# Up tiles of the SwiGLU parts as block products, and another place for the w_ada dot products

## The chip, the core and the metric

The kernel runs on one core of a Trainium2 chip. The core's engines work side by side, each on its own instruction stream: TensorE (PE; its weight loads are listed apart as PEld), VectorE (DVE), ScalarE (ACT), GpSimd (POOL) and SyncE (SP, which issues nearly all DMAs here). The metric is device time in microseconds. A profiled execution gives a trace beside it.

## What is computed

Two layers of a streaming encoder on x of 512 positions by 1024 features, all in float32. Each layer has three sub-layers, each behind a norm whose shift, scale and gate come from the vector c:

```python
c_act = silu(c)
for l in range(2):
    mod = (c_act @ w_ada[l] + b_ada[l]).reshape(B, 9, 1024)
    h = modulate(rms_norm(x, norm_gain[l, 0]), mod[:, 0], mod[:, 1])
    x = x + 0.5 * mod[:, 2] * swiglu(h, w_gate[l, 0], w_up[l, 0], w_down[l, 0])
    h = modulate(rms_norm(x, norm_gain[l, 1]), mod[:, 3], mod[:, 4])
    x = x + mod[:, 5] * hybrid_mixer(h, ...)
    h = modulate(rms_norm(x, norm_gain[l, 2]), mod[:, 6], mod[:, 7])
    x = x + 0.5 * mod[:, 8] * swiglu(h, w_gate[l, 1], w_up[l, 1], w_down[l, 1])

def swiglu(h, w_gate, w_up, w_down):
    return (silu(h @ w_gate) * (h @ w_up)) @ w_down
```

w_gate and w_up are 1024 x 2816, w_down is 2816 x 1024. The mixer has three branches (A: attention with a learned bias, B: pooling over trailing windows, C: attention with forget gates); each branch's output goes through its own matrix and a sigmoid gate that is itself a product of h, the three are summed, and an output product follows. `mod` is 9216 dot products of length 1024 in each layer.

## The kernel before

**Numbers in two halves.** Each float32 operand of a product is split into a high half (a rounded copy, made by ScalarE) and a low half (the rest, one subtraction on VectorE). `triple` (line 117) then does three matmuls for one product: high by high, high by low, low by high.

**Weights.** `wchunk` (262) brings one 512 KB weight tile: a load into one of two "raw" buffers from SP's queue, the split into one of three "whi" tiles on ScalarE (277) and one of three "wlo" tiles on VectorE (279).

**SwiGLU.** `Ffn.run` (595) handles the 22 tiles of 128 hidden features in three parts of 6, 8 and 8 tiles. Each part makes its hidden tiles ("acts") from gate and up products, then its share of the down product (`k_outer`, 388) with the residual in `residual_tail` (430). A tile of gate or up done alone is `unit` (577): 8 x 3 matmuls of 512 columns. In parts 1 and 2, gate tiles go in pairs through `seven` (507): the pair's weights are seen as 2 x 2 blocks and so is h, and seven block products stand for eight, by Winograd's form of Strassen's scheme. That is 7 x 4 x 3 = 84 matmuls of 256 columns for two tiles (`add_product`, lines 128 to 130). Beside them it needs sums of weight blocks (522 to 525), their splits, and folds of partial results (538 to 549) in a tile "c". The sums and "c" live in the four buffers tagged "v2" (the profile writes "v"). The sums of h's blocks are made once for each sub-layer by `Blocks` (454), during part 0. The up tiles go through `seven` only where there is no next phase (`nxt is None`), that is in the last SwiGLU of layer 1; in the other three they are two `unit`s.

**The w_ada dot products.** `mod_step` (200) does 128 of the 9216 outputs of a layer: a 512 KB load from SP's queue into a "v2" buffer, one multiply-and-sum against silu(c) on VectorE (206), and one small instruction for a scale or a gate. silu(c), spread over all partitions, lies in `silc`, a "b" buffer. There are 144 steps; 16 are done in the kernel's first product, and 128 stand in `mod_queue`. They are taken out at a rate: each weight tile asks `side_work` (251) first.

```python
elif side and in_ffn[0] and mod_tag[0] == "v2":
    mod_credit[0] += MOD_RATE[0]
    while mod_credit[0] >= 1.0:
        mod_credit[0] -= 1.0
        mod_pop()
```

So nothing is taken while `in_ffn` is false (the mixer) or the tag is "raw" (the down product of a SwiGLU's last part). `mod_need(l, j)` (231) takes out at once what is still missing up to output group j of layer l. It is called where results are needed: by each phase's `prefetch` (the next phase's norm), and ahead of each down product (its gate).

**The mixer.** `Mixer.run` (1114): projections, attention A, attention C with the merge of branch A as filler, then branch B's `pool_front` (1025) four times and the merge of branch C (`merge_units`, 1068), the merge of branch B, and the output product. Branch C's values lie in the four "v2" buffers until its attention ends, and the low and high halves of the merged result take them from the merge of branch B on. GpSimd adds the branches up (1149). In layer 0, `silc` is loaded again after the attentions (1168 to 1170); in layer 1 it is not.

**Order.** The program states each engine's instructions; a scheduler puts them in a fixed order for each engine ahead of the run, ready instructions by their place in the program. A "b" tile takes one of 17 buffers.

Of the kernel before, what the change touches and what calls it, by code (L numbers as in the profile page):

```python
# [15 lines left out]
F32 = mybir.dt.float32  # L16
# [6 lines left out]
P = 128  # L23
T = 512
D = 1024
# [3 lines left out]
L = 2  # L29
# [11 lines left out]
def encoder_kernel(tc, xT, c, w_ada, b_ada, gains, w_gate, w_up, w_down, w_qkv, w_f, w_ubg,  # L41
                   qk_gain, rel, fbias, w_pool, pool_scale, w_branch, w_out, inv_cnt, w_first, out):
    nc = tc.nc
# [14 lines left out]
    NB, NRAW = 17, 2  # L58
# [5 lines left out]
    def st(shape, dt, tag, bufs):  # L64
        return sb.tile(shape, dt, tag=tag, bufs=bufs, name=nm(tag))
# [4 lines left out]
    def mmt(shape=(P, T)):  # L70
        return ps.tile(list(shape), F32, tag="mm", bufs=4, name=nm("mm"))
# [66 lines left out]
    silc = [st([P, D], F32, "b", NB)]  # L138
    sil_dram = dr.tile([1, D], F32, name="sil_dram")
# [84 lines left out]
    mod_tag = ["v2"]  # L224
# [6 lines left out]
    def mod_need(l, j):  # L231
        while mod_ptr[0] < min(len(mod_queue), (l * 9 + j + 1) * 8 - 16):
            mod_pop()

    MOD_RATE = [1.0]
    in_ffn = [True]
# [325 lines left out]
    class Ffn:  # L562
# [32 lines left out]
        def run(self, nxt):  # L595
            l, s, ms = self.l, self.s, self.ms
            in_ffn[0] = True
            mod_tag[0] = "v2"
            parts = ((0, 6), (6, 8), (14, 8))
            for part, (f0, nf) in enumerate(parts):  # L600
                acts = []
                n = 0
                if part == 0 and self.norm is None:
                    acts = self.start()
                    n = 3
                    blocks = Blocks()
                elif part == 0:
                    g0, u0, g1 = self.pre
                    pg, pu, pg1 = mmt(), mmt(), mmt()
                    for hs in range(2):  # L610
                        self.norm.back(hs, acc if hs else mmt)
                        cols = slice(hs * HALF, (hs + 1) * HALF)
                        if hs == 0:
                            later(FRONT1, lambda: self.norm.front(1, acc))
                            later(BACK1, lambda: self.norm.back(1, acc))
                        for k in range(KD):
                            self.unit(pg, g0, cols, (k,))
                            self.unit(pu, u0, cols, (k,))
                        self.unit(pg1, g1, cols)
                    u1 = self.gate_up(1, 1)  # L620
                    acts.append(self.act(0, pg, pu))
                    pu1 = mmt()
                    self.unit(pu1, u1)
                    acts.append(self.act(1, pg1, pu1))
                    n = 2
                    blocks = Blocks(self.norm.xa, modc[:, l, 3 * ms])
                if part == 0:
                    blocks.schedule(T_FIRST, T_STEP)
                elif part == 1:
                    blocks.finish()  # L630
                MOD_RATE[0] = 0.5 if part else 1.0
                while part and n < nf:
                    both = [apply(p, AF.Silu)
                            for p in seven([w_gate[l, s, f0 + n + i] for i in range(2)], blocks, acc)]
                    ups = seven([w_up[l, s, f0 + n + i] for i in range(2)], blocks, mmt) if nxt is None else None
                    for i, sg in enumerate(both):
                        if ups is not None:
                            pu = ups[i]
                        else:
                            u = self.gate_up(1, f0 + n + i)  # L640
                            pu = mmt()
                            self.unit(pu, u)
                        acts.append(self.act(n + i, None, pu, sg))
                    n += 2
                while n < nf:
                    g = self.gate_up(0, f0 + n)
                    u = self.gate_up(1, f0 + n)
                    pg, pu = mmt(), mmt()
                    self.unit(pg, g)
                    self.unit(pu, u)  # L650
                    acts.append(self.act(n, pg, pu))
                    n += 1
                mod_need(l, 3 * ms + 2)
                MOD_RATE[0] = 1.75
                for c0 in (0, T):
                    def src(c):
                        r0 = (f0 + 2 * c) * P
                        return w_down[l, s, r0:r0 + 2 * P, c0:c0 + T].rearrange("(k p) c -> p k c", p=P)

                    def ops(hi, lo, kt, j):  # L660
                        return (hi[:, j * P:(j + 1) * P], lo[:, j * P:(j + 1) * P],
                                acts[kt][:, 0, :], acts[kt][:, 1, :])

                    last = part == len(parts) - 1
                    if last and c0 == 0 and nxt is not None:
                        nxt.prefetch("v2")
                        mod_tag[0] = "raw"
                    split = last and c0 > 0
                    hook = None
                    if split:  # L670
                        hook = nxt.prefetch_weights if nxt is not None else (lambda: None)
                    for j, hs, o in k_outer(src, nf // 2, ops, hook):
                        d = c0 // P + j
                        residual_tail(d, hs, o, modc[:, l, 3 * ms + 2, d:d + 1], nxt if last else None)
                        if last and nxt is None:
                            cols = slice(0, T) if hs is None else slice(hs * HALF, (hs + 1) * HALF)
                            nc.sync.dma_start(out[:, d, cols], xd(d)[:, cols])
# [382 lines left out]
    def wpool_load(l):  # L1060
        raw = st([P, 4, P], F32, "t1", 2)
        nc.sync.dma_start(raw, w_pool[l].rearrange("g c e -> c g e"))
        w = st([P, 2, 4, P], F32R, "pta", 1)
        split_to(w[:, 0], w[:, 1], raw)
        return w[:, 0], w[:, 1]
# [32 lines left out]
    def drain(*gens):  # L1098
        for it in gens:
            for _ in it:  # L1100
                pass

    class Mixer:
# [1 line left out]
            self.l = l  # L1105

        def prefetch(self, xtag):
            mod_need(self.l, 5 if self.l + 1 < L else 8)
            self.norm = Norm(self.l, 1, xtag)

        def prefetch_weights(self):
# [2 lines left out]
        def run(self, nxt):  # L1114
# [50 lines left out]
            finish_turns()  # L1165
            turns.clear()
            poll(True)
            if l + 1 < L:
                silc[0] = st([P, D], F32, "b", NB)
                nc.sync.dma_start(silc[0], sil_dram.broadcast_to([P, D]))  # L1170
            wp = wpool_load(l)
            mc = merge_units(l, 2, yc, put_c)
            for gi in range(4):
                b = pool_front(l, gi)
                later(60, lambda gi=gi, b=b: pool_back(l, gi, b, wp, yb))
            drain(mc)
            poll(True)
            mb = merge_units(l, 1, yb, put_b)
            drain(mb)
# [87 lines left out]
```

## Time and profile before

| | |
|---|---|
| median of three runs | 2421.05 us (2418.97 to 2422.55) |
| span of the profiled execution | 2419.9 us |
| PE busy | 2380.5 us, 98% |
| VectorE busy | 1596.5 us, 66% |
| ScalarE busy | 1129.6 us, 47% |
| DMA | 320.27 MB, mean 132 GB/s |
| w_ada dot products (line 206) | 144, 188.0 us on VectorE |

A row of the profile that groups instructions gives the line of the kernel, the engine, the operation, what is written and what is read, shapes, a count, the busy time with the mean of one, and the idle time of the engine ahead of them with what ended it. A row in the order of time begins with start and length. A row of a stretch gives start and end, its length, then for each engine the busy time and the number of records, the granted TensorE clock, the DMA engines' busy share and GB/s. Matmuls are pipelined, so the distance of their starts tells their rate, not the length of one.

### The profile page before, as it was taken

Reading aid. Unit: us, or ns where it says so; the run is one execution under the profiler, and the core shown is the slowest. Engines: PE = TensorE matmul, PEld = TensorE weight load, DVE = VectorE, ACT = ScalarE, POOL = GpSimd, SP = SyncE. Lnnn points to the kernel's source line nnn. Section 1 sums busy time; section 2 is a strip of 40 time slices with the busy share of each in tenths; the row PEclk is TensorE's granted clock in tenths of the full one; section 3 lists DMA queues with packets and bytes.
Section 4 is the critical chain, followed back from the end, with each engine's and each line's share of the span. In section 5 each row is a group of like instructions: output and inputs, shape, how many; then the busy total and the mean of one; then the engine's idle time right before and its main releaser. Section 6 shows DMA issues by size and latency. Waiting matters only on the chain. (4 is left out here: it accounts for less than half of the span.)

```text
span 2419.9 us, 34577 instructions
## 1 busy us (share of the span) xinstructions
PE 2380.5 (98%) x13242; PEld 2061.8 (85%) x13242; DVE 1596.5 (66%) x2830; ACT 1129.6 (47%) x1946; POOL 342.8 (14%) x423
## 2 busy tenths in 40 slices
PE   7999999999999999999999999999999999999999
PEld 5888988778878898989898889888788888989898
DVE  8977756787643378777567766467866434658583
ACT  5342444786632353424443424457765333536362
POOL 3000001144432210000000000111454322000000
PEclk9999999999999999999999999999999999999999
DMA  7746443223323436464326443423233234133233
GB/s 272 243 157 235 158 137 98 93 70 111 104 91 113 139 98 242 158 235 157 131 79 214 171 163 105 140 70 101 86 100 104 96 108 145 65 100 103 95 103 104
DMA packets 116282, 320.27 MB, mean 132 GB/s; under 512 B 11122, under 2 KB 13298, under 8 KB 116116
## 3 DMA queue, kind: packets, MB, share of 16 engines
q1 hardware_dynamic: 114962, 313.86, 39.0%
q0 software_dynamic: 1152, 4.19, 0.4%
q8 instruction: 104, 1.70, 0.3%
q14 instruction: 62, 0.51, 0.1%
q10 hardware_dynamic: 2, 0.00, 0.0%
HBM read 311.64 MB, written 6.38 MB: 131 GB/s over the span
## 5 line engine op out<-in xcount | busy, mean ns | idle before, releaser
L277 ACT CAST whi<-raw 128x1024 fp32r<-128x1024 f32 (+1 forms) x315 | 327.7, 1044 | 573.5 <-PE acc L120 275.0
L279 DVE TENSOR_TENSOR wlo<-raw,whi 128x1024 fp32r<-128x1024 f32 x307 | 378.4, 1235 | 261.9 <-ACT whi L277 258.5
L119 PE MATMUL acc<-b,whi 128*128 128x512 f32 (+1 forms) x960 | 360.6, 376 | 0.0
L121 PE MATMUL acc<-b,wlo 128*128 128x512 f32 (+1 forms) x960 | 356.8, 372 | 0.8 <-DVE wlo L279 0.8
L120 PE MATMUL acc<-b,whi 128*128 128x512 f32 (+1 forms) x960 | 356.9, 372 | 0.0
L119 PE MATMUL mm<-hhi,whi 128*128 128x512 f32 x664 | 259.2, 391 | 1.4 <-ACT whi L277 1.4
L120 PE MATMUL mm<-hlo,whi 128*128 128x512 f32 x664 | 258.7, 390 | 0.0
L121 PE MATMUL mm<-hhi,wlo 128*128 128x512 f32 x664 | 258.1, 389 | 0.0
L206 DVE CUSTOM_DVE_ANT_0 v<-v,b,badac 128x1024 f32<-128x1024 f32 x144 | 188.0, 1316 | 32.9 <-DMA v<-in_w_ada_dram 32.7
L121 PEld LDWEIGHTS acc<-b,wlo 128*128 128x128 f32 x960 | 180.8, 188 | 32.6 <-DVE wlo L279 1.2
L119 PEld LDWEIGHTS acc<-b,whi 128*128 128x128 f32 x960 | 180.8, 188 | 31.6 <-DVE xv L434 0.3
L120 PEld LDWEIGHTS acc<-b,whi 128*128 128x128 f32 x960 | 180.9, 188 | 30.2
L119 PE MATMUL acc<-hhi,whi 128*128 128x512 f32 x480 | 191.0, 399 | 3.9 <-ACT whi L277 2.2
L120 PE MATMUL acc<-hlo,whi 128*128 128x512 f32 x480 | 188.3, 392 | 0.5 <-DVE hlo L717 0.5
L121 PE MATMUL acc<-hhi,wlo 128*128 128x512 f32 x480 | 188.0, 392 | 0.0
L119 PEld LDWEIGHTS mm<-hhi,whi 128*128 128x128 f32 x664 | 125.0, 188 | 27.5 <-ACT whi L277 2.3
L121 PEld LDWEIGHTS mm<-hhi,wlo 128*128 128x128 f32 x664 | 124.6, 188 | 26.2
L120 PEld LDWEIGHTS mm<-hlo,whi 128*128 128x128 f32 x664 | 124.7, 188 | 24.8
L119 PE MATMUL acc<-whi,hhi 128*128 128x512 f32 x336 | 137.8, 411 | 0.8 <-DVE xv L385 0.8
L121 PE MATMUL acc<-whi,hlo 128*128 128x512 f32 x336 | 132.0, 393 | 0.0
L120 PE MATMUL acc<-wlo,hhi 128*128 128x512 f32 x336 | 131.7, 392 | 0.0
L590 DVE TENSOR_TENSOR t<-mm,t 128x512 f32<-128x512 f32 (+1 forms) x78 | 51.7, 662 | 103.9 <-PE mm L121 102.6
(314 smaller groups left out, 5507.4 us busy)
## 6 DMA issues: line engine op xcount, KB each, us to landing
v<-in_w_ada_dram SPq DMA_DIRECT2D x144, 512.0 KB, 5.4
raw<-in_w_down_dram SPq DMA_DIRECT2D x88, 512.0 KB, 3.5
raw<-in_w_up_dram SPq DMA_DIRECT2D x82, 512.0 KB, 3.5
raw<-in_w_gate_dram SPq DMA_DIRECT2D x79, 512.0 KB, 3.8
raw<-in_w_ubg_dram SPq DMA_DIRECT2D x56, 512.0 KB, 3.4
raw<-in_w_qkv_dram SPq DMA_DIRECT2D x42, 512.0 KB, 3.7
raw<-in_w_branch_dram SPq DMA_DIRECT2D x24, 512.0 KB, 3.5
raw<-in_w_out_dram SPq DMA_DIRECT2D x16, 512.0 KB, 3.5
```

The source lines that it names most:

```text
L119: mm(o, lh, rh, start=start, stop=False)
L120: mm(o, lh, rl, start=False, stop=False)
L121: mm(o, ll, rh, start=False, stop=stop)
L206: dot = nc.vector.tensor_tensor_reduce(out=raw, in0=raw, in1=silc[0], scale=1.0, scalar=badac[:, l, j, d:d + 1], op0=ALU.mult, op1=ALU.add ...
L277: nc.scalar.copy(hi, raw)
L279: lo_eng.tensor_tensor(lo, raw, hi.bitcast(F32), op=ALU.subtract)
L590: nc.vector.tensor_tensor(pr[:, cols], p, sg[:, cols], op=ALU.mult)
```

## The change

In the three SwiGLU sub-layers that have a next phase, the up tiles of parts 1 and 2 now go in pairs through `seven` as well. The rate at which dot products are taken out goes from 0.5 to 0 in the gate and up products of parts 1 and 2, and from 1.75 to 1.25 in the down products; in part 0 it stays 1. The mixer's `prefetch` asks only for group 5 in both layers (before, group 8 in layer 1). `silc` is loaded again in layer 1 too. Around the pool fronts and the merge of branch C, `in_ffn` is true with rate 1, so that each of their weight tiles takes one dot product out.

```diff
-                MOD_RATE[0] = 0.5 if part else 1.0
+                MOD_RATE[0] = 0.0 if part else 1.0
                 while part and n < nf:
                     both = [apply(p, AF.Silu)
                             for p in seven([w_gate[l, s, f0 + n + i] for i in range(2)], blocks, acc)]
-                    ups = seven([w_up[l, s, f0 + n + i] for i in range(2)], blocks, mmt) if nxt is None else None
+                    ups = seven([w_up[l, s, f0 + n + i] for i in range(2)], blocks, mmt)
                     for i, sg in enumerate(both):
-                        if ups is not None:
-                            pu = ups[i]
-                        else:
-                            u = self.gate_up(1, f0 + n + i)
-                            pu = mmt()
-                            self.unit(pu, u)
-                        acts.append(self.act(n + i, None, pu, sg))
+                        acts.append(self.act(n + i, None, ups[i], sg))
                     n += 2
...
                 mod_need(l, 3 * ms + 2)
-                MOD_RATE[0] = 1.75
+                MOD_RATE[0] = 1.25
...
         def prefetch(self, xtag):
-            mod_need(self.l, 5 if self.l + 1 < L else 8)
+            mod_need(self.l, 5)
...
             poll(True)
-            if l + 1 < L:
-                silc[0] = st([P, D], F32, "b", NB)
-                nc.sync.dma_start(silc[0], sil_dram.broadcast_to([P, D]))
+            silc[0] = st([P, D], F32, "b", NB)
+            nc.sync.dma_start(silc[0], sil_dram.broadcast_to([P, D]))
             wp = wpool_load(l)
+            in_ffn[0] = True
+            mod_tag[0] = "v2"
+            MOD_RATE[0] = 1.0
             mc = merge_units(l, 2, yc, put_c)
...
             drain(mc)
+            in_ffn[0] = False
             poll(True)
```

## The prediction

> **What bounds the kernel now.** I read the page first, then the stretches of the SwiGLU parts, then their edges in the order of time, then the dot products in the same stretches, and last the waits.
>
> ```profile
> span 2419.9 us, 34577 instructions
> PE 2380.5 (98%) x13242; PEld 2061.8 (85%) x13242; DVE 1596.5 (66%) x2830; ACT 1129.6 (47%) x1946; POOL 342.8 (14%) x423
> PEclk9999999999999999999999999999999999999999
> ```
>
> PE is busy in 2380.5 of 2419.9 us, at an unchanged clock. So only less work on PE can shorten the kernel, and only a new gap on PE can lengthen it. The change touches six stretches, parts 1 and 2 of three SwiGLU sub-layers. The fourth sub-layer, the last one, already runs the form that the six are to get. Here are all eight in order, the last sub-layer in the last two rows.
>
> ```profile
> core 0: us, PE busy (x) PEld busy (x) DVE busy (x) ACT busy (x) POOL busy (x), PEclk, DMA share, GB/s
> 126.07:210.70 84.63, 83.78 (x529) 76.02 (x528) 64.29 (x100) 35.79 (x57) 0.00 (x0) 1.00 0.55 190
> 254.22:337.74 83.52, 83.52 (x529) 75.94 (x528) 55.94 (x83) 36.09 (x57) 0.00 (x0) 1.00 0.45 152
> 969.12:1052.64 83.52, 83.52 (x529) 75.94 (x528) 62.26 (x99) 35.53 (x57) 0.00 (x0) 1.00 0.56 190
> 1096.16:1179.68 83.52, 83.52 (x529) 75.94 (x528) 55.94 (x83) 35.75 (x57) 0.00 (x0) 1.00 0.44 153
> 1325.21:1410.18 84.97, 83.78 (x529) 76.01 (x528) 64.97 (x101) 35.77 (x57) 0.00 (x0) 1.00 0.54 187
> 1453.70:1537.22 83.52, 83.52 (x529) 75.94 (x528) 47.22 (x62) 35.61 (x57) 0.00 (x0) 1.00 0.33 109
> 2167.51:2247.83 80.32, 80.32 (x674) 79.96 (x672) 66.84 (x101) 46.70 (x81) 0.00 (x0) 1.00 0.36 112
> 2291.38:2371.46 80.08, 80.08 (x673) 79.95 (x672) 66.94 (x100) 46.65 (x81) 0.00 (x0) 1.00 0.36 113
> ```
>
> The first column is the length of the part's gate and up products. In a 528-matmul part, four pairs alternate 84 matmuls of 256 columns (gate) with 48 of 512 (up). In a 672-matmul part all eight groups are of 84. PE has no gap in any of them but the first and the fifth, whose gate product waits once for ScalarE's copy:
>
> ```profile
> 132.78 0.38 PE L128 MATMUL acc<-b,ptb 128*128 128x256 f32 x1 [0.85 <-ACT v L542]
> 1332.26 0.39 PE L128 MATMUL acc<-b,ptb 128*128 128x256 f32 x1 [1.19 <-ACT v L542]
> ```
>
> **The up tiles.** First and last starts of one gate group and one pair of up tiles, third part:
>
> ```profile
> 969.12 0.28 PE L128 MATMUL acc<-hhi,whi 128*128 128x256 f32 x1
> ...
> 979.10 0.40 PE L119 MATMUL mm<-hhi,whi 128*128 128x512 f32 x1
> ...
> 1052.64 0.39 PE L119 MATMUL acc<-b,whi 128*128 128x512 f32 x1
> ```
>
> A group of 84 takes 979.10 - 969.12 = 9.98 us, or 119 ns a matmul. The part of 83.52 us is four such groups and four times two up tiles, so these take (83.52 - 39.92) / 4 = 10.90 us, or 227 ns a matmul. Half a 512-column matmul would be 113.5 ns: seven products in place of eight promise 12.5%, but each short matmul costs some 5 ns extra, and the gain shrinks to 0.92 us a pair, 3.68 us a part. The last sub-layer shows what arrives of it: 83.52 - 80.32 = 3.20 us in its part 1 and 83.52 - 80.08 = 3.44 us in its part 2. I take these measured values rather than 3.68, since they hold the small delays that a fuller VectorE and ScalarE cause: 3 x 3.20 + 3 x 3.44 = **19.9 us less**. The first and fifth parts' excess (84.63 - 83.52 and 84.97 - 83.52, together 2.6 us) I leave where it is; if it went, the gain would be 22.5 us, the far end on that side.
>
> The row of the stationary loads in such a group is
>
> ```profile
> L128 PEld LDWEIGHTS acc<-b,ptb x384: 186/188/192, 128.8 to 2358.1; 128*128 128x128 f32 x192
> ```
>
> [...]
>
> **VectorE and ScalarE in those parts.** The seven products need sums, splits and folds that single tiles don't. By the table VectorE goes to 66.9 of 80 us, ScalarE to 46.7. This is hidden as long as VectorE has its 13 us left. The dots compete for just these:
>
> ```profile
> core 0: us, DVE busy (x), PEclk, DMA share, GB/s
> 126.07:210.70 84.63, 16.45 (x25) 1.00 0.55 190
> 254.22:337.74 83.52, 8.93 (x14) 1.00 0.45 152
> 969.12:1052.64 83.52, 15.50 (x25) 1.00 0.56 190
> 1096.16:1179.68 83.52, 9.01 (x14) 1.00 0.44 153
> ```
>
> A dot leaves two records, so about 12 dots lie in part 1 and 7 in part 2; one costs 1.3 us. With the rate at 0, only dots that the down product before left over run there: credit in part 1 was 8, so 4 of the 12 were leftovers, and at 1.25 in place of 1.75 fewer are. Four left over are 5 us of VectorE's 13. What can be late is the first up group of a part, prepared beside these leftovers: from nothing to one wait such as the two above (1.2 us), in three parts. I take nothing to 0.3 each, since the first gate group already shows that wait only twice in eight.
>
> **The dots' new places.** Counting credits by the code: 8 dots by the end of the first part 0, 15 and 25 after the next downs; then the mixer's prefetch needs 32, so 7 are issued at once at the end of part 2; the merges of branch C and its pool fronts have 16 weight chunks at rate 1, so 48; then 4 and 4 in part 0 as now (56), 64, 74; in layer 1's first sub-layer 4 and 2 (80), 87, 97, again 7 at once (104), 16 beside the merges (120), and 4 and 4 in part 0 of the last sub-layer (128). Each brings a 512 KB load on SP's queue.
>
> The 7 at once: their results are gates that only the output product uses, and the down product behind them is light. The nearest rows are the bulk that sub-layer two already has:
>
> ```profile
> 912.30 1.77 SPq L203 DMA_DIRECT2D v<-in_w_ada_dram  x4
> 917.08 0.38 SPq L266 DMA_DIRECT2D raw<-in_w_down_dram  x1
> 920.02 5.26 SPq L203 DMA_DIRECT2D v<-in_w_ada_dram  x4
> 925.37 0.39 SPq L266 DMA_DIRECT2D raw<-in_w_down_dram  x1
> ```
>
> and what PE and VectorE did around it (first row), beside VectorE's load in the down product after a part 2 (second) and in the merges of both layers (third, fourth):
>
> ```profile
> core 0: us, PE busy (x) PEld busy (x) DVE busy (x) ACT busy (x) POOL busy (x), PEclk, DMA share, GB/s
> 881.00:936.40 55.40, 55.40 (x272) 46.99 (x271) 46.88 (x73) 26.34 (x36) 0.00 (x0) 1.00 0.68 231
> 337.74:376.06 38.32, 38.32 (x236) 34.57 (x235) 17.50 (x20) 17.92 (x26) 8.44 (x8) 1.00 0.44 150
> 672.27:770.00 97.73, 97.73 (x432) 80.76 (x432) 39.21 (x49) 31.00 (x42) 29.09 (x29) 1.00 0.29 94
> 1870.72:1968.50 97.78, 97.78 (x433) 80.82 (x433) 39.31 (x49) 30.99 (x42) 29.09 (x29) 1.00 0.29 94
> ```
>
> Bursts of 4 loads between two weight loads, VectorE at 85%, 231 GB/s: no gap on PE. Seven dots (9 us) against 21 idle us of VectorE in the second row are hidden too; without that cover they would cost 9 us each time. I take 0.
>
> The merges: 16 dots are 21 us more on VectorE, 60 of 98, and 16 x 0.52 MB over 98 us is 86 GB/s more, 180 in all. Both are below the first row. The weights have slack there, since ScalarE's split waits not for the data but for PE to free the split tile:
>
> ```profile
> 714.94 1.05 ACT L277 CAST whi<-raw 128x1024 fp32r<-128x1024 f32 x1 [4.39 <-PE acc L120]
> 723.10 1.05 ACT L277 CAST whi<-raw 128x1024 fp32r<-128x1024 f32 x1 [6.61 <-PE acc L120]
> ```
>
> The dots' tiles ("v") hold branch C's values until the attention ends, so the first loads start just there, four at a time, among the pool fronts' weights. PE's wait at that spot is the same with a reload of the c vector (layer 0) and without it (layer 1, which gets it now):
>
> ```profile
> 669.19 0.63 PE L972 MATMUL mm<-ident,t 128*128 128x128 f32 x4 [1.52 <-DVE t L960]
> 1867.62 0.63 PE L972 MATMUL mm<-ident,t 128*128 128x128 f32 x4 [1.50 <-DVE t L960]
> ```
>
> So the reload is free. For the loads I take nothing to 1.5 us a layer, nearer to nothing. The 8 dots in the last sub-layer's part 0 meet what the first row above shows for the second sub-layer: 0. Lower rates in the downs take VectorE work out of gapless stretches: 0.
>
> **Sum.** Against the profiled execution: 2419.9 - 19.9 + 1 (starts of parts and merges together) = 2401 us of span. The median of the runs, 2421.05, lies 1.15 us above this span, so the forecast is **2402 us**; the small terms reach from 0 to 3 x 1.2 + 2 x 1.5 = 6.6 us, its own range is 2398 to 2408.
>
> **Rivals.** (B) *The edges leak.* Each of the six parts stalls its first up group by 1.2 us, and each merge phase by 1.5: 10.2 us in place of 1, **2411 us**. For it: the two waits quoted, in parts that begin with leftover dots. Against it: the last sub-layer shows none at either start.
>
> (C) *VectorE becomes the bound.* If all of the 12 dots of a part 1 stayed there, VectorE would have 66.9 + 16 = 83 us of work in an 80 us part, and the parts would take 83.5 us as now: **2421 us**, no change. This also stands for a change that doesn't thin out those parts as it says. Against it: rate 0 leaves leftovers alone.
>
> (D) *SP's queue, slower.* A dot's load waits at the head of SP's queue for a free "v" tile, and the weights of the merges queue behind it.
>
> ```profile
> SPq L203 <- DVE modc L206: 51.4, 33, 5.8
> ```
>
> Such waits exist: 33, 1.56 us on average. If each of the 32 loads beside the merges held up a weight chunk by that, uncovered, it would cost 50 us: 2421 - 20 + 50 = **2451 us**. It decides from 0.62 us uncovered a load (20/32). Against it: the 4.4 to 6.6 us that the splits wait for PE are cover for a wait of 1.56 and for most of 5.8.
>
> **Chances and range.** Forecast 0.74, B 0.15, C 0.05, D 0.06. What a measurement can tell from no change is 0.2%, or 4.8 us. Forecast and B are faster by more: 0.89; C is the same: 0.05; D is slower: 0.06. For eight in ten I take the forecast with its bounds and the nearer part of B: from 2397.5, a microsecond beyond the far end of 22.5 us gained, to 2412.
>
> **What would show it.** Six stretches of 672 matmuls and 80 to 81 us; groups of 84 at 9.98 us also in "mm" banks; no new PE wait over 1.5 us between 650 and 830 us nor in layer 1's merges; about 16 dots there; SP's waits before L203 longer without a PE wait behind them. I am wrong if a part with 672 matmuls takes over 82 us, if PE waits for L277 or L279 in the merges or after part 2, or if VectorE's idle time in those parts falls near nothing.

## The result, and the profile after

| | median us | lowest to highest | runs | span of the profiled execution |
|---|---|---|---|---|
| before | 2420.43 | 2418.11 to 2422.55 | 10 | 2419.9 |
| after | 2412.34 | 2408.73 to 2416.84 | 10 | 2410.1 |

The ratio is 0.9971, with a 95% interval of 0.9961 to 0.998: 8.1 us less by the medians, 9.8 us by the two spans. 2402 us was predicted, and 2397.5 to 2412 as the range. The page of after:

```profile
span 2410.1 us, 36817 instructions
PE 2363.2 (98%) x14106; PEld 2088.6 (87%) x14106; DVE 1729.5 (72%) x3070; ACT 1199.8 (50%) x2090; POOL 353.3 (15%) x423
PEclk9999999999999999999999999999999999999999
```

By this page nothing is wrong: PE is at 98% as before and the clock row reads 9 throughout. A slice of 60 us hides a few microseconds at half clock, as will be seen. The six parts with the new form, by stretches:

```profile
core 0: us, PE busy (x) PEld busy (x) DVE busy (x) ACT busy (x) POOL busy (x), PEclk, DMA share, GB/s
124.94:205.98 81.04, 80.32 (x674) 79.96 (x673) 70.24 (x107) 46.72 (x80) 0.00 (x0) 1.00 0.39 127
249.52:329.36 79.84, 79.84 (x674) 79.83 (x673) 70.04 (x108) 46.71 (x80) 0.00 (x0) 1.00 0.39 126
966.84:1046.67 79.83, 79.83 (x673) 79.82 (x672) 70.38 (x109) 46.89 (x80) 0.00 (x0) 1.00 0.41 133
1090.22:1170.15 79.93, 79.93 (x674) 79.89 (x672) 67.20 (x101) 46.92 (x81) 0.00 (x0) 1.00 0.34 117
1315.54:1395.59 80.05, 80.05 (x673) 79.88 (x672) 69.84 (x107) 46.79 (x80) 0.00 (x0) 1.00 0.38 128
1439.14:1519.11 79.97, 79.97 (x674) 79.89 (x672) 69.82 (x107) 46.80 (x80) 0.00 (x0) 1.00 0.37 126
```

They add up to 480.66 us, where the same six took 503.68: 23.0 us gained. Two parts of the last sub-layer, unchanged in form, give 0.7 more (79.83 us each). So some 14 us of 23.7 were lost again. Two rows of TensorE's timeline, one in each layer, carry most of it:

```profile
686.50 0.80 PE L121 MATMUL acc<-hhi,wlo 128*128 128x512 f32 x1 [3.95 <-DVE wlo L279]
1878.72 0.50 PE L121 MATMUL acc<-hhi,wlo 128*128 128x512 f32 x1 [3.91 <-DVE wlo L279]
```

Both lie beside the pool fronts, where the moved dots begin. First the same 27 us of layer 0 before, then after, with the two places at half clock:

```profile
672.27:699.50 27.23, 27.23 (x122) 22.42 (x122) 13.16 (x22) 10.46 (x16) 14.26 (x20) 1.00 0.27 86
```

```profile
663.24:690.50 27.26, 23.31 (x95) 18.77 (x95) 23.45 (x33) 9.69 (x15) 14.09 (x16) 0.90 0.64 238
685.30:692.10 6.80, 5.60 (x13) 4.44 (x14) 6.77 (x8) 2.75 (x4) 4.51 (x6) 0.50 0.47 167
1879.90:1883.30 3.40, 3.40 (x10) 2.63 (x9) 3.40 (x4) 0.69 (x1) 3.26 (x4) 0.50 0.76 299
```

PE was gapless there and is now idle for 4 us, while VectorE goes from 48% to 86%. At each wait the granted clock falls to 0.50, for 6.8 us in layer 0 and 3.4 us in layer 1. At half clock PE was busy for 5.60 + 3.40 us. Matmuls of 512 columns start 0.43 us apart there (layer 0, 687.09 to 691.36 us) and 0.23 us apart behind it (692.16 to 694.92), so by estimate half of that, 4.5 us, comes on top of the 7.9 us of waiting.

A third loss is in the down products after part 2. The one of layer 1 before, then both after:

```profile
1537.22:1575.53 38.31, 38.31 (x235) 34.56 (x234) 17.50 (x20) 17.92 (x26) 8.28 (x8) 1.00 0.44 148
```

```profile
329.36:368.89 39.53, 38.77 (x237) 34.68 (x235) 23.57 (x35) 18.55 (x27) 8.48 (x8) 1.00 0.62 212
1519.11:1559.10 39.99, 38.87 (x237) 34.70 (x236) 23.77 (x37) 18.56 (x27) 8.26 (x8) 1.00 0.61 210
```

They are 1.2 and 1.7 us longer. Here the chain does not start on VectorE. SP's queue in layer 0, and ScalarE's next split of a down weight:

```profile
318.64 12.40 SPq L203 DMA_DIRECT2D v<-in_w_ada_dram  x7
331.15 0.89 SPq L266 DMA_DIRECT2D raw<-in_w_down_dram  x2
```

```profile
337.52 1.05 ACT L277 CAST whi<-raw 128x1024 fp32r<-128x1024 f32 x1 [4.90 <-DMA raw<-in_w_down_dram]
```

The loads of the seven dots taken at once hold SP's queue for 12.4 us, and the next down weights are loaded behind them. Their first split comes 8.2 us after the end of the part (337.52 - 329.36); before, one stood right there (337.76, the part ending at 337.74). PE's waits of 0.4 to 0.8 us follow some 24 us later, for the split of a down weight that waits for its load as well. VectorE idles there: 4.27 us ahead of the subtraction that PE waits for in layer 0. The account of the spans: -23.7 + 7.9 + 4.5 + 2.9 = -8.4. Measured are -9.8; the last -1.4 us are many small differences that I did not follow up.

**Why PE waits.** VectorE's timeline of layer 0 up to the wait (small instructions left out):

```profile
672.97 2.05 DVE L279 TENSOR_TENSOR wlo<-raw,whi 128x1024 fp32r<-128x1024 f32 x1
674.94 2.06 DVE L206 CUSTOM_DVE_ANT_0 v<-v,b,badac 128x1024 f32<-128x1024 f32 x1
...
677.69 1.27 DVE L206 CUSTOM_DVE_ANT_0 v<-v,b,badac 128x1024 f32<-128x1024 f32 x1
...
679.50 2.06 DVE L279 TENSOR_TENSOR wlo<-raw,whi 128x1024 fp32r<-128x1024 f32 x1
681.48 2.06 DVE L206 CUSTOM_DVE_ANT_0 v<-v,b,badac 128x1024 f32<-128x1024 f32 x1
...
684.46 0.18 DVE L1037 TENSOR_TENSOR hd<-strip,icnt 128x16 f32<-128x16 f32 x1 [0.92 <-POOL strip L1033]
...
685.23 1.22 DVE L279 TENSOR_TENSOR wlo<-raw,whi 128x1024 fp32r<-128x1024 f32 x1
```

and the two of ScalarE that belong to it, of which the first makes that weight's high half:

```profile
678.85 1.05 ACT L277 CAST whi<-raw 128x1024 fp32r<-128x1024 f32 x1
...
685.40 0.62 ACT L384 CAST ptb<-ssum 128x512 fp32r<-128x512 f32 x1 [4.90 <-DVE ssum L1040]
```

The weight's low half, for which PE waits, could have been made from 679.90 on. It begins at 685.23, because VectorE's order has a weight subtraction, a dot and a pool step ahead of it, and the pool step waits for GpSimd. Besides, all of this is slow. The dot takes 2.06 instead of 1.27 us and the subtraction 2.05 instead of 1.22. GpSimd's window additions are slower too, first before, then after:

```profile
L1039 POOL TENSOR_TENSOR strip<-strip 128x512 f32<-128x512 f32 x12 | 13.0, 1080 | 0.5
```

```profile
L1033 POOL TENSOR_TENSOR strip<-strip 128x512 f32<-128x512 f32 x12 | 23.1, 1921 | 0.5
```

And the dots are not spread over the merge, as their rate of one a weight tile suggests. The dots' own records in the first part 1, then in these first 27 us and in the next 70:

```profile
core 0: us, DVE busy (x), PEclk, DMA share, GB/s
124.94:205.98 81.04, 3.78 (x6) 1.00 0.39 127
663.24:690.50 27.26, 12.19 (x14) 0.90 0.64 238
690.50:761.00 70.50, 12.39 (x18) 0.99 0.43 147
```

With two records each, 7 of 16 dots lie in the first 27 us.

### The profile page after: what moved, and what is told of

Same layout as the page of the kernel before. It is cut to its first block, busy times and chain, and to the rows that moved or that the text cites. A ratio compares the mean times of both kernels' runs of the same rounds, so it can differ in the third digit from the quotient of the medians.

```text
span 2410.1 us, 36817 instructions
## 1 busy us (share of the span) xinstructions
PE 2363.2 (98%) x14106; PEld 2088.6 (87%) x14106; DVE 1729.5 (72%) x3070; ACT 1199.8 (50%) x2090; POOL 353.3 (15%) x423
## 5 line engine op out<-in xcount | busy, mean ns | idle before, releaser
L277 ACT CAST whi<-raw 128x1024 fp32r<-128x1024 f32 (+1 forms) x267 | 277.4, 1043 | 449.1 <-PE acc L120 258.6
L279 DVE TENSOR_TENSOR wlo<-raw,whi 128x1024 fp32r<-128x1024 f32 x259 | 323.5, 1252 | 208.4 <-ACT whi L277 205.7
L206 DVE CUSTOM_DVE_ANT_0 v<-v,b,badac 128x1024 f32<-128x1024 f32 x144 | 195.4, 1365 | 40.2 <-DMA v<-in_w_ada_dram 40.1
L385 DVE TENSOR_TENSOR ptb<-v,ptb 128x1024 fp32r<-128x1024 f32 x128 | 156.6, 1224 | 35.7 <-ACT ptb L384 34.3
L384 ACT CAST ptb<-v 128x1024 fp32r<-128x1024 f32 x128 | 134.0, 1050 | 93.0 <-DVE v L452 46.4
L384 ACT CAST whi<-raw 128x1024 fp32r<-128x1024 f32 (+1 forms) x128 | 106.8, 834 | 97.9 <-PE acc L120 50.3
L385 DVE TENSOR_TENSOR wlo<-raw,whi 128x1024 fp32r<-128x1024 f32 (+1 forms) x128 | 121.9, 952 | 7.0 <-ACT whi L384 5.2
L121 PEld LDWEIGHTS acc<-hhi,wlo 128*128 128x128 f32 x480 | 91.4, 190 | 29.0 <-DVE wlo L279 9.8
L434 DVE SCALAR_TENSOR_TENSOR xv<-acc,modc,xv 128x512 f32<-128x512 f32 (+1 forms) x112 | 76.9, 690 | 50.0 <-PE acc L121 50.0
L329 POOL TENSOR_TENSOR ssum<-ssum,t 128x256 f32<-128x256 f32 (+1 forms) x45 | 46.7, 1037 | 445.7 <-ACT t L328 445.6
```

The costliest lines, as they stand in the source:

```text
L121: mm(o, ll, rh, start=False, stop=stop)
L206: dot = nc.vector.tensor_tensor_reduce(out=raw, in0=raw, in1=silc[0], scale=1.0, scalar=badac[:, l, j, d:d + 1], op0=ALU.mult, op1=ALU.add ...
L277: nc.scalar.copy(hi, raw)
L279: lo_eng.tensor_tensor(lo, raw, hi.bitcast(F32), op=ALU.subtract)
L384: nc.scalar.copy(hi, src)
L385: nc.vector.tensor_tensor(lo, src, hi.bitcast(F32), op=ALU.subtract)
```

## The experiments

From the comparison my theory was: in the fixed order the dots stand ahead of weight subtractions and pool steps, and VectorE and GpSimd slow each other there; PE's wait then costs again by the clock. The rivals: the dots' loads hold up the weights (rival D); the pool fronts alone are the wrong place; the loss comes from the seven products. Each run is beside runs of before on the same chip. "Waits" are PE's longest beside the fronts and merges of each layer, and "halved" is the time at clock 0.5 behind them.

| run | us | before beside it | ratio, 95% | waits, us | halved, us |
|---|---|---|---|---|---|
| after | 2412.34 | 2420.43 | 0.9971 (0.9961 to 0.998) | 3.95, 3.91 | 6.83, 3.41 |
| sevens only | 2424.04 | 2421.05 | 1.0014 (1.0005 to 1.0023) | | |
| moved dots only | 2430.94 | 2421.05 | 1.0039 (1.0025 to 1.0052) | 3.94, 3.95 | 6.83, 3.41 |
| no pool additions | 2398.48 | 2422.32 | one run | none over 1.5 | none |
| loads without dots | 2398.55 | 2422.32 | one run | none over 1.5 | none |
| dots without loads | 2422.65 | 2422.32 | one run | 4.96, 4.96 | 6.83, 6.83 |
| dots taken after the fronts | 2413.55 | 2422.32 | 0.9963 (0.9949 to 0.9977) | 4.78, 4.54 | 6.83, 3.41 |
| down rate 1.75 | 2412.79 | 2421.05 | 0.9964 (0.995 to 0.9978) | 3.95, 4.21 | 6.83, 6.83 |
| both of these | 2411.55 | 2421.05 | 0.996 (0.9948 to 0.9973) | 4.52, 4.60 | 6.83, 3.41 |
| c vector in PSUM | 2409.46 | 2420.27 | 0.9956 (0.9942 to 0.997) | 2.51, 2.52 | 6.83, 3.41 |
| same, down rate 1.75 | 2408.23 | 2420.27 | 0.9946 (0.9932 to 0.996) | 2.52, 2.35 | 3.41, 3.41 |
| dots held behind the fronts | 2412.79 | 2420.27 | 0.9966 (0.9954 to 0.9978) | 2.62, 2.62 | 6.83, 6.83 |
| dots behind their own weight | 2401.43 | 2421.30 | 0.9921 (0.9907 to 0.9936) | none over 1.5 | none |
| own weight, from the first front | 2406.12 | 2421.30 | 0.9936 (0.9919 to 0.9952) | 1.00, 1.04 | 3.41 after part 2 |
| own weight, down rate 1.75 | 2399.72 | 2421.30 | 0.9913 (0.9898 to 0.9928) | none over 1.5 | none |

**The two halves of the change.** Before, with only the up tiles by `seven` and every dot where it was:

```diff
-                    ups = seven([...], blocks, mmt) if nxt is None else None
+                    ups = seven([...], blocks, mmt)
...
-                        acts.append(self.act(n + i, None, pu, sg))
+                        acts.append(self.act(n + i, None, ups[i], sg))
```

> The kernel before with the up tiles by seven products in all later parts, and the dot products where they were (rate 0.5 in those parts, 1.75 in the down products, none beside the merges). If VectorE has no room for both (67 us of the seven form and 16 us of dots in a part 1 of 80 us), the three parts 1 stay near 83 us, the parts 2 near 80.5, PE has waits in them, and the time is 2408 to 2412. If VectorE's order bears it, all parts take 80 to 80.5 us and the time is 2398 to 2400, since nothing is added to the merges; then moving the dots bought nothing.

3.0 us slower than before by the medians (the profiled execution is the fastest of its ten). Two of its parts 1:

```profile
125.91:211.56 85.65, 82.02 (x674) 80.44 (x672) 77.97 (x128) 45.35 (x80) 0.00 (x0) 1.00 0.51 164
968.34:1053.79 85.45, 81.74 (x674) 80.32 (x673) 75.92 (x124) 45.55 (x80) 0.00 (x0) 1.00 0.48 159
```

VectorE is at 91 and 89%, and the parts are longer than the 84.63 and 83.52 us of before. The seven products gain nothing while the dots stay. The other half is after with the up tiles as single ones again.

> The changed kernel with the up tiles as two single tiles, as before, in the three sub-layers: the dots' new places alone. If the moved dots cost what the changed kernel's trace shows (waits of 3.9 us in each merge phase, halved clock of 6.8 and 3.4 us, 1 to 2 us at each end of part 2), it is 2430 to 2434 us, 10 to 14 more than the kernel before. If the loss comes from the up products themselves, it is 2420 to 2423.

9.9 us slower, with the same two waits as after to a few hundredths of a microsecond. The loss beside the merges therefore belongs to the moved dots, not to the seven products. The gain is in neither half: one alone costs 3.0, the other 9.9, and together they save 8.1 us.

**Which part of the moved work.** First, branch B's window additions are left out, so that GpSimd has none of them:

```diff
-            nx = st([P, T + 16], F32, "strip", 2)
-            nc.gpsimd.memset(nx[:, :16], 0.0)
-            nc.gpsimd.tensor_tensor(nx[:, 16:], cur[:, 16:], cur[:, 16 - step:T + 16 - step], op=ALU.add)
-            cur = nx
```

> The changed kernel without GpSimd's additions in the pool fronts (branch B's window sums are left out, the dots stay). [...] If the number of dots ahead of the subtraction is enough by itself, a wait of 2 to 3 us stays. If loads are the cause, 3.9 us stays.

Second, the 16 loads of each layer stay, but their dots are cut to the first column, so that these outputs of w_ada are not computed:

```diff
-            dot = nc.vector.tensor_tensor_reduce(out=raw, in0=raw, in1=silc[0], scale=1.0,
+            k = 1 if lean[0] else D
+            dot = nc.vector.tensor_tensor_reduce(out=raw[:, :k], in0=raw[:, :k], in1=silc[0][:, :k], scale=1.0,
```

> The changed kernel, where each dot product of the merge phases is cut to its first column (the rest of the sum is left out), with its 512 KB load kept. Theory Q: no PE wait over 1.5 us beside the pool fronts, clock 1.0, some 2400 us of span. Theory L: the waits of 3.9 us stay, about 2410.

Third, the reverse: full dots, of the c vector with itself instead of with w_ada, and none of the 16 loads.

```diff
-        with after("dma"):
-            nc.sync.dma_start(raw, w_ada[l, j, d])
+        if not lean[0]:
+            with after("dma"):
+                nc.sync.dma_start(raw, w_ada[l, j, d])
...
-            dot = nc.vector.tensor_tensor_reduce(out=raw, in0=raw, in1=silc[0], scale=1.0,
+            dot = nc.vector.tensor_tensor_reduce(out=raw, in0=silc[0] if lean[0] else raw, in1=silc[0], scale=1.0,
```

> The changed kernel, where the dot products of the merge phases take the c vector twice and their 512 KB loads are left out. Theory Q: the PE wait stays, less what VectorE stood waiting for the first load (2 us), so 1.5 to 4 us, with dots of 2.06 us beside GpSimd's additions. Theory L: the waits go, and the span falls to about 2400 us.

Without the additions, and without the dots' work, the time is 2398.5 us and no wait over 1.5 us is left beside the fronts and merges (one run each). The second of these in the stretch of the fronts:

```profile
663.00:690.00 27.00, 27.00 (x124) 22.37 (x123) 16.98 (x40) 10.57 (x16) 13.57 (x20) 1.00 0.78 279
```

279 GB/s, more than the 238 of after, and PE has no gap: loads and SP's queue are not the cause here. With dots and no loads the waits come back and are longer (4.96 us, also longer than the 1.5 to 4 us expected): dots that no longer wait for data go ahead in greater number, 9 of them between 663 and 690.5 us where after has 7. Rival D falls beside the merges. Leaving the additions out also shortens the path from front to pool step, so that run alone does not tell the slowing from the order.

**Is it the place?** The dots were taken from the queue behind the four fronts in the program, at a rate of 1.34 so that all 16 are still taken.

```diff
-            in_ffn[0] = True
-            mod_tag[0] = "v2"
-            MOD_RATE[0] = 1.0
             mc = merge_units(l, 2, yc, put_c)
...
+            in_ffn[0] = True
+            mod_tag[0] = "v2"
+            MOD_RATE[0] = 1.34
             drain(mc)
```

> The changed kernel, but the 16 dot products of each merge phase start only behind the four pool fronts (12 weight tiles at a rate of 1.34 in place of 16 at 1). Theory Q (dots stand ahead of the weights' subtractions on VectorE while GpSimd's pool additions run): the PE waits of 3.95 and 3.91 us for wlo L279 go, the clock stays at 1.0 there, and the time falls by 2 x 3.9 us of waits and about 5 us of halved clock to some 2400 us. Theory L (the extra loads crowd SP's queue and the DMA engines wherever they are): the waits only move into the merges, a wait of over 2 us stays, and the time stays at 2408 to 2413. Theory E (the loss lies at the ends of part 2, in the seven dots issued at once): 2411 as it is.

No different from after: the scheduler, which lets ready instructions go ahead, put them among the fronts again. The wait has only moved: PE waits until 697.42 for VectorE's reading of an accumulator (line 1051), which has a pool step and two dots ahead of it:

```profile
689.50 2.06 DVE L206 CUSTOM_DVE_ANT_0 v<-v,b,badac 128x1024 f32<-128x1024 f32 x1
...
691.49 2.05 DVE L206 CUSTOM_DVE_ANT_0 v<-v,b,badac 128x1024 f32<-128x1024 f32 x1
...
695.86 0.18 DVE L1037 TENSOR_TENSOR hd<-strip,icnt 128x16 f32<-128x16 f32 x1 [2.31 <-POOL strip L1033]
...
696.62 0.75 DVE L1051 SCALAR_TENSOR_TENSOR b<-acc,psc,b 128x512 fp32r<-128x512 f32 x1
```

VectorE itself idles for 2.31 us there, for additions that take longer beside the dots: 1.90 and 1.86 us (at 690.56 and 692.59 us), where the median of before is 1.04.

So the dots were next held behind the last front by the fixed order itself, on top of that edit:

```diff
-        split_to(b[:, 0, :], b[:, 1, :], df)
+        nc.scalar.copy(b[:, 0, :], df)
+        last["norm"] = nc.vector.tensor_tensor(b[:, 1, :], df, b[:, 0, :].bitcast(F32), op=ALU.subtract).ins
```

> As the run with the dots behind the pool fronts, but with VectorE's order fixed: each dot of the merge phases must stand behind the last pool front's split. (In that run's trace the dots had been put among the fronts again.) If the place beside GpSimd's additions is the cause: no PE wait over 1.6 us there, clock 1.0, 2398 to 2402. If the dots cost the same anywhere beside the merges: 2408 to 2414.

Again no gain. The fronts are now free, and the dots come all at once behind them, five ahead of one weight's subtraction (the last of them, the subtraction, and the reading of an accumulator behind it):

```profile
697.62 2.32 DVE L206 CUSTOM_DVE_ANT_0 v<-v,b,badac 128x1024 f32<-128x1024 f32 x1
...
699.86 1.22 DVE L279 TENSOR_TENSOR wlo<-raw,whi 128x1024 fp32r<-128x1024 f32 x1
...
702.21 0.74 DVE L1052 SCALAR_TENSOR_TENSOR b<-acc,psc,b 128x512 fp32r<-128x512 f32 x1
```

PE waits 2.62 us for line 1052 and then 1.12 for a subtraction in layer 0, 2.62 and 1.61 in layer 1. The pool fronts are not the cause by themselves: in both places dots gather ahead of what PE needs next from VectorE.

**The seven taken at once.** After, with the old rate in the down products (`MOD_RATE[0] = 1.25` to `1.75`), so that no dots are missing at the end of part 2.

> The changed kernel with the rate of 1.75 in the down products, so that no seven dots are left to be issued at once at the ends of part 2 and fewer in the last sub-layer. If that burst costs the 1.2 and 1.7 us seen there, 3 us less than the changed kernel: 2408 to 2410. If it costs nothing, the same 2412. If the fuller down products fill VectorE at the start of part 1, waits come up there and it is slower than 2412.

The waits after part 2 are gone, and so is the jam on SP's queue: four loads of down weights go out from 316.30 us on with no dot's load among them. But layer 1's wait now halves the clock for 6.83 us instead of 3.41, which is chance, as shown under the clock below, and the median is the same as that of after. Together with the dots taken after the fronts:

> Both repairs: merge dots behind the pool fronts at rate 1.34, and 1.75 in the down products. If the two losses are what separates the changed kernel from the bare gain of 22.5 us, 2396 to 2400 us. If a loss remains elsewhere, above 2402.

2411.55 us, still the waits beside the merges.

**Is it the slowing?** Here the c vector is copied into two PSUM banks, and each dot is done in two halves with one operand from there. If the slowing of VectorE and GpSimd by each other were the whole loss, I expected no wait over 1.6 us and 2399 to 2402 us.

```diff
+                half = st([P, 1], F32, "dot", 4)
+                for i in range(2):
+                    dot = nc.vector.tensor_tensor_reduce(out=raw[:, i * T:(i + 1) * T], in0=silp[i],
+                                                         in1=raw[:, i * T:(i + 1) * T], scale=1.0, ...)
...
+            for i in range(2):
+                silp.append(mmt())
+                nc.scalar.copy(silp[i], silc[0][:, i * T:(i + 1) * T])
```

> The changed kernel, where the merge phases read the c vector from two PSUM banks and each dot product is done in two halves, so that VectorE's dots have one operand in SBUF in place of two; number, loads and places of the dots stay. [...] Theory N (the number of dots in VectorE's queue is enough): VectorE has even a little more to do, PE waits of 2 to 5 us and a halved clock stay, time 2408 to 2414.

The halves take 733 to 753 ns, all 64 of them. GpSimd's additions take 1.04 us at the least, and 1.98, 1.90 and 1.85 us (at 678.27, 685.21 and 687.24 us) where they meet a weight subtraction, which still has two SBUF operands:

```profile
L211 DVE CUSTOM_DVE_ANT_0 v<-mm,v,dot 128x512 f32<-128x512 f32 x32 | 23.6, 746 | 0.2
L1043 POOL TENSOR_TENSOR strip<-strip 128x512 f32<-128x512 f32 x12 | 18.2, 1515 | 0.5
```

The long waits fall from 3.9 to 2.5 us each. So neither the slowing nor the number of dots explains the loss alone: the slowing is a part of it, not all. With rate 1.75 in the down products as well:

> The run with the c vector in PSUM, and 1.75 in the down products so that no seven dots come at once after part 2. [...] Theory N: 2406 to 2412.

2408.23 us; the waits of 2.5 and 2.4 us remain.

**The order itself.** If dots ahead of subtractions are the cause, each dot should go behind the subtraction of the weight tile that takes it out. On top of the edit that takes the dots after the fronts, `wchunk` names its own subtraction as what the next dot has to follow. The dot's load then stands behind that weight's load too, but loads alone had cost nothing here.

```diff
-        side_work(side)
+        if not paced[0]:
+            side_work(side)
...
-            lo_eng.tensor_tensor(lo, raw, hi.bitcast(F32), op=ALU.subtract)
+            lo_ins = lo_eng.tensor_tensor(lo, raw, hi.bitcast(F32), op=ALU.subtract).ins
+        if paced[0]:
+            last["norm"] = lo_ins
+            side_work(side)
```

> The run with the dots behind the pool fronts, but each dot of the merges is taken out behind the weight tile it is counted with, and VectorE must do that tile's subtraction first: dots can no longer gather ahead of a subtraction. If the gathering is what made the wait (so far 3 to 5 us in every form with dots in a bunch), no PE wait over 1.6 us stays in the fronts and merges, clock 1.0, time 2397 to 2401. If dots beside the merges cost the same however they are spread, 2408 to 2414.

2401.43 us. From the first front to the end of branch C's merge, in after and then in this run:

```profile
663.24:760.06 96.82, 92.87 (x398) 76.22 (x398) 61.95 (x86) 28.77 (x39) 31.77 (x28) 0.96 0.49 172
```

```profile
663.10:754.16 91.06, 90.58 (x398) 74.24 (x398) 60.75 (x86) 28.85 (x39) 31.48 (x28) 1.00 0.53 183
```

The same 398 matmuls take 91.1 us instead of 96.8 (before, without the dots, 90.0). VectorE does nearly the same work, 61 us instead of 62, and DMA moves as much. But PE loses 0.5 us instead of 4, at full clock. VectorE's timeline:

```profile
671.25 1.23 DVE L282 TENSOR_TENSOR wlo<-raw,whi 128x1024 fp32r<-128x1024 f32 x1 [0.46 <-ACT whi L280]
672.39 2.06 DVE L206 CUSTOM_DVE_ANT_0 v<-v,b,badac 128x1024 f32<-128x1024 f32 x1
```

Dots still run beside the additions and still take 2.06 us. But each subtraction now waits only for its own high half, and the slow dot falls into time that VectorE spent waiting for GpSimd before (3.21 us in this row of before):

```profile
690.73 0.17 DVE L1043 TENSOR_TENSOR hd<-strip,icnt 128x16 f32<-128x16 f32 x1 [3.21 <-POOL strip L1039]
```

The same rule from the first front on, at rate 1:

> The same rule for the dots, but from the first pool front on and at rate 1, so four dots stand beside GpSimd's pool additions. [...] If only the gathering mattered, as the run before: 2397 to 2401.

2406.12 us, above the range given, though not because of the fronts: they keep waits of only 1.00 and 1.04 us, which do not halve the clock. But two waits in the down product after layer 0's part 2, of 1.19 and 0.76 us and close together, do, for 3.41 us. With the rate of 1.75 in the down products on top of the rule after the fronts:

> Dots behind their own weight, after the fronts, and rate 1.75 in the down products: no burst after part 2 either. If both losses are then gone, 2395 to 2399, the full gain of the seven products; if the fuller down products take as much as the bursts did, the same as the run without the rate.

2399.72 us, 21.6 less than before and the best of all. Its span of 2396.6 lies 23.3 us below that of before: nearly the whole gain of the parts, with no wait over 1.5 us beside the merges or after part 2.

**The clock.** To see what an idle PE costs by itself, before was given eight waits of graded size, in the down products of parts 0 and 1. A tiny product is copied by ScalarE, goes through GpSimd operations of chosen widths and feeds another tiny product, behind which the next 60 triples are held. The outputs don't depend on it.

```diff
+    def stall():
+        ...
+        mm(o, ident, ones[:, :2], start=True, stop=True)
+        nc.scalar.copy(t[:, :2], o)
+        for n in stalls.pop(0):
+            nc.gpsimd.tensor_scalar(t[:, :n], t[:, :n], 1.0, None, op0=ALU.mult)
+        pin[:] = mm(mmt((P, 2)), t[:, :P], ones[:, :2], start=True, stop=True).ins, 60
```

> The kernel before, with eight waits put into TensorE's stream in the down products of parts 0 and 1, each a round by ScalarE and GpSimd of growing length (some 2 to 5.5 us); the results are unchanged. If an idle stretch of TensorE alone brings the halved clock, it comes behind the longer of these waits and not behind the shorter, with the edge between 1.5 us (no halved clock in any trace so far) and 3.9 us (always one). If the halved clock had another cause in the merge phases, all eight leave it at 1.0.

> The kernel before with eight waits of some 1.5 to 2.4 us put into TensorE's stream, finer steps than in the run before (there 2.4 us already halved the clock for 3.4 us); the results are unchanged. If a single length decides, the halved clock comes behind all waits over one value between 1.6 and 2.4 us and behind none below it; if what was done shortly before counts too, the order by length is broken.

| wait of PE, us | time at clock 0.5 behind it, us |
|---|---|
| 1.57 | none |
| 1.57, 1.79, 1.84, 2.42, 2.44, 2.59, 2.60, 2.91 | 3.41 each |
| 2.92, 3.58, 4.96, 5.07, 5.31, 6.53 | 6.83 each |
| 5.55 | 10.24 |

Why did one of the two waits of 1.57 us, both in the shorter series, halve the clock and the other not? Within a trace the clock changes only at whole multiples of 3.413 us from one another: the two halvings of after, which begin at 685.26 and 1879.92 us, lie 350 of them apart. So time can be cut into slots of that length. The first wait of 1.57 us (114.27 to 115.84 us) falls across two slots, the second (238.48 to 240.05) into one:

```profile
111.53:114.95 3.42, 2.75 (x14) 2.22 (x12) 3.42 (x5) 0.21 (x2) 0.34 (x1) 1.00 0.79 247
114.95:118.36 3.41, 2.52 (x12) 2.15 (x13) 3.18 (x7) 0.80 (x1) 0.84 (x1) 1.00 0.39 132
237.83:241.24 3.41, 1.84 (x11) 1.53 (x10) 0.89 (x1) 1.10 (x2) 0.37 (x1) 1.00 0.80 285
241.24:244.65 3.41, 3.41 (x10) 2.64 (x9) 1.61 (x4) 0.00 (x0) 0.00 (x0) 0.50 0.24 64
```

From the first full clock on, the traces of all runs have 12510 such slots at full clock, and 34 of them were followed by half clock: all 33 in which PE idled 1.73 us or more, none with 1.52 us or less, and between these one slot with 1.57 us was and one with 1.69 us was not. So in these traces what decides is the idle time of PE within one slot, with the edge between 1.52 and 1.73 us of 3.413, and not the length of a wait. In the run from the first front on, the two short waits after part 2 add up to 1.73 us in one slot. A wait of 3.9 us can bring 3.41 or 6.83 us of half clock, depending on where it falls.

The eight longer waits add up to 36.0 us and cost 56.7 us (2476.94 - 2420.27); the eight shorter ones to 17.6 us and 33.3 (2454.64 - 2421.30). So in these two runs, of one execution each, the waits cost 1.6 to 1.9 times their own length.

## Why the prediction was wrong

**The step that failed** is the one on the merges: "For the loads I take nothing to 1.5 us a layer, nearer to nothing." It came out at 3.9 us of waiting a layer, 7.9 in all, with 4.5 us of lost clock on top. The reasons given for it were sums over 98 us, VectorE at 60 and DMA at 180 GB/s, and the price was put on the loads. The sums were right. But 7 of 16 dots came in the first 27 us, and VectorE's order had them ahead of subtractions that PE needed. The loads, which the step priced, cost nothing there: with loads and hardly any dots no such wait was left. The cover quoted, the 4.4 to 6.6 us for which ScalarE's splits wait for PE, was read at 714 and 723 us, behind the fronts. In the fronts ScalarE waits for VectorE's pool step instead (4.90 us in the row at 685.40), and a delay on VectorE is passed on through both engines.

**The clock** was a term that the sum did not have. The reading of before, "at an unchanged clock", was taken over, and nothing asked what a wait would do to it.

**Seven at once after part 2** were taken as 0, by VectorE's 21 idle us in that down product. They cost 1.2 and 1.7 us, and the waits went with the rate of 1.75. The prediction asked for room on VectorE, and VectorE had it. What failed is the cover on SP's queue: the bulk of sub-layer two that it compared has a weight load behind every four loads of dots, while here seven stand in a row for 12.4 us ahead of the down weights. No run takes the seven loads and their dots apart, but the trace leads from PE's wait to a late load. The bound given for lost cover, 9 us each, was far too high.

**The up tiles** were right in kind and low in size: 19.9 taken, 22.5 at the far end, 23.0 measured. The parts reached 79.8 to 80.1 us, better than the model parts of before (80.32 and 80.08), and the fifth part's excess, which I had left where it was, went from 1.45 to 0.2 us (80.05). That of the first part stayed: 81.04 us, 1.2 more than the 79.84 of the second. Loads and products overlap in the new form too: by the rows of line 128 in after a load takes 188 to 192 ns (medians, in "acc" and "mm" banks), yet a part of eight groups, four of them in "mm" banks, takes 79.84 us, or 9.98 a group and 119 ns a matmul.

**The parts' starts** were right: PE idles 0.7 us in the first part (81.04 - 80.32, one wait for ScalarE's copy) and nowhere else, where nothing to 0.3 us for each was taken. By the first part's row in the fence of the dots' records (6 of them), 3 leftover dots run in it, where the prediction had fewer than 4. VectorE's load of 67 to 70 us agrees with the 66.9 plus leftovers.

**The c vector's reload** showed no wait of its own in layer 1, as said: PE waits 1.51 us at that spot (1852.37 us), and 1.50 before.

**The rivals.** B named 2411 us and was near the measured time, but by chance, since the places are others: it had six part starts stall and the merges lose 1.5 us each; the starts did not, and the merges lost four times as much with the clock. C's mechanism is real, but in the half-change only: with the dots left in the parts VectorE is at 88 to 91% of them and the time is 2424 us. That this is near the 2421 given is partly luck. Only the parts 1 have the 12 dots that C counts, so by its own terms the parts 2 would still have gained some 10 us; measured, the parts 1 take 85.5 to 85.7 us, more than C's 83.5, and the parts 2 83.7, 81.9 and 79.8. That moving the dots is what makes the seven products pay was rightly seen. D falls beside the merges, by both runs on the loads, but its mechanism, a dot's load ahead of weights on SP's queue, is the one seen after part 2. SP's wait ahead of these loads grew from 51.4 us, as the prediction's last part expected, to 62.6 in after (the row below) and 60.9 in the run with loads alone, where no PE wait stands behind it beside the merges:

```profile
SPq L203 <- DVE modc L206: 62.6, 35, 5.8
```

What was to show the prediction wrong, "PE waits for L277 or L279 in the merges or after part 2", is just what the trace of after has.

## What to carry to other kernels

Before work is put beside a stage that "has room", read the fixed order of each engine in its first microseconds, not the sum over the stage: what counts is how many fillers can stand ahead of one instruction that TensorE needs. Tie each filler behind that instruction (here each dot behind its weight's subtraction) rather than choose another place or rate for it. Look at the DMA queue in the same way: a bulk of loads taken at once delays the weights behind it. And price a wait of TensorE that can bring the halved clock above its own length: at 1.6 to 1.9 times in the two series here.

## What the hardware showed that I had not expected

**Short waits halve TensorE's clock.** What counts in these traces is how long PE idles within one slot of 3.413 us: from 1.73 us on always, up to 1.52 us never, and once each way between. Then the clock is halved for 3.41, 6.83 or 10.24 us, whole slots. Two waits of 1.19 and 0.76 us were enough as well, where they fell into one slot with 1.73 us, and a wait of 1.57 us was not where it fell across two. Equal waits met the slots differently, so a part of the price is chance: 3.95 us brought 6.83 us of half clock and 3.91 us brought 3.41.

**Two SBUF operands on VectorE beside GpSimd.** Beside GpSimd's additions a dot of 1024 columns takes 2.06 us instead of 1.27 and a subtraction 2.05 instead of 1.22. GpSimd's addition of 512 columns goes from 1.08 to 1.92 us (means of 12). Halves of a dot with one operand in PSUM stay at 0.75. No run shows by what the two engines hinder each other. In the run with dots behind their own weights the slowing is there and PE loses 0.5 us in that stage; it hurts where TensorE's next operand stands behind it, as in after, where PE waits 3.95 and 3.91 us.
